# Dividing 2-D attention by its softmax sums after the value product, with the factors passed through DRAM

## The chip, the cores and the metric

The kernel runs on one core of one Trainium2 chip. That core has five engines with a queue of instructions each: TensorE (PE in the profile: matrix products and transposes; PEld is its weight loads), VectorE (DVE), ScalarE (ACT), GpSimd (POOL) and SyncE (SP, which here only issues transfers). Transfers between DRAM and the on-chip memory run on 16 DMA engines. An engine takes its instructions in order; an instruction that must wait holds up all behind it on its engine. The metric is device time in microseconds (us), lower is better.

## The reference

One encoder block on 1024 positions of width 1024, in float32. After a modulated norm, one projection gives queries, keys and values for two attention branches and two gates. Branch A is a dilated attention with 8 heads, branch B a 2-D neighbourhood attention with 8 heads of width 64. Their outputs are projected, gated, added and projected again; then come a second norm, a ConvFFN and a last norm. The change is in branch B:

```python
def neighbourhood_attention_2d(q, k, v, rpb):
    ...                       # rows = 16, GRID_W = 64; a window of 8 rows x 16 columns, clamped to the grid
    s = jnp.einsum('brqhd,brakhd->bhrqak', q5, kr).astype(jnp.float32) * scale + bias[None]
    s = jnp.where(col_mask[:, None, :], s, -jnp.inf)
    p = jax.nn.softmax(s, axis=(-2, -1))
    o = jnp.einsum('bhrqak,brakhd->brqhd', p.astype(v.dtype), vr)
    return o.reshape(B, S, H, Dh)
```

The softmax is an exponential divided by its sum over a query's keys. Since the sum is one number for each query and head, the division can be made in p or, with the same result up to rounding, in o.

## The kernel before, in words

Products of full accuracy are made from split operands: a float32 number is the sum of a high part (`hi`) and a low part (`lo`), and a product is three matmuls, hi\*hi, hi\*lo and lo\*hi (lines 84 to 86 in `product`). ACT makes a high part by copying, DVE or POOL the low part by subtracting.

The attention of both branches is written out slot by slot. A slot is one pass of the loop at line 1378 over `slots[s]`, 0 to 101; within a slot the phases run in the order `settle`, early, first, O, T, one step of fill, S, last, and the rest of the fill. Jobs are put in by `at(slot, phase, job)`; `later(n, job)` puts a job in the early phase n slots on. All five engines follow this written order here (lines 851 and 853). The fill is another task, the projections of the gates (`fill_steps`, line 1318): three matmuls a step (lines 84 to 86), two steps a slot up to slot 63, three in slots 64 to 95, one in slots 96 to 101, and 17 more after the last slot (line 1443). Work of other engines that has no fixed place (output sums, splitting of values and weights) goes through `aside`, which hands it out by a credit of 550 ns for each fill step; `ensure` forces it out when it is needed.

The 2-D heads run in slots 64 to 101: head h starts at slot s0 = 64 + 4h (`NaHead`, line 1207). The queries are cut into four column blocks `cb` of 16 columns (256 queries each) and two halves R of 128 queries, and a block has 288 or 384 keys for a half. For each head:

- slots s0 to s0+3, phase S: `scores` of blocks 0, 3, 1, 2 (line 1260, PE). The next slot's `settle` runs `soft`: DVE adds the bias and takes the maximum (line 1270), ACT takes the exponential and its sum (line 1272; the sum lands in `st[:, 1]`).
- two slots after its scores, phase first: `normalise` (line 1275) of that block: DVE takes the reciprocal of two columns of sums (line 1277), then half R = 0 is multiplied on POOL and half R = 1 on DVE (line 1280), in place in P.
- slots s0+4 to s0+7, phase T: `turn` transposes P on PE (line 1289) into one of two PSUM banks `T`; the next `settle` splits it, high part on ACT (line 878), low part on DVE (line 882), which frees the bank.
- slots s0+7 and s0+9, phase O: `out` multiplies with the values (line 930, PE). Its two halves are added into the output tile `oT` by ACT (line 1309) and DVE (line 1313). A tile `oT` holds two heads, on partitions 0 to 63 and 64 to 127; after the second head it goes to DRAM (`o_scr`, line 1315), from where the next stage loads it (`o_load`, line 1411, tile `oraw`).

SP issues the loads in the same written order: for the next heads the queries and keys (line 402), values (line 777) and bias (line 1248), for the fill the weights (line 65) and the store of its results (line 1327), for branch A its last factors (lines 1145 to 1203, up to slot 85). POOL has, beside line 1280, the low parts of the values (line 784) and of the fill's weights (line 962) and the weighting of branch A (lines 1193 and 1201).

After the slots come the gated products (`pj<-o0hi,whi` in the profile) and the ConvFFN. Behind line 1543, where the written order ends, a planner that simulates the engines' times orders most engines anew, with some stretches written out again.

Of the kernel before, what the change touches and what calls it, by code (L numbers as in the profile page):

```python
# [10 lines left out]
FT = mybir.dt.float32  # L11
FR = mybir.dt.float32r
AF = mybir.ActivationFunctionType
OP = mybir.AluOpType
# [3 lines left out]
S = 1024  # L18
# [10 lines left out]

def hybrid_encoder(tc, xT, c, w_ada, small, w_in, p1_bias, p23_bias, na_bias, ln2_mult, ident, w_br, w_out,  # L30
                   w_up, w_down, out):
    nc = tc.nc
    act, dve, pool, pe, sp = nc.scalar, nc.vector, nc.gpsimd, nc.tensor, nc.sync
# [3 lines left out]
    dram = tc.alloc_tile_pool(name="scr", bufs=1, space=DRAM)  # L37
# [89 lines left out]
    early = tc.alloc_tile_pool(name="early", bufs=1, reuse_waits="tile")  # L127
# [9 lines left out]
    later = itertools.cycle([(adapool, "wada", 4)] * 4 + [(early, "wada", 3)] * 3)  # L137
# [143 lines left out]
    g_scr = dram.tile([16, 128, S], FT, name="gs")  # L281
    st_scr = dram.tile([4, 64, 128], FT, name="sts")
    f_scr = dram.tile([4, 2, 2, 8, S], FT, name="fcs")
    o_scr = [dram.tile([4, 128, S], FT, name=n) for n in ("oa", "ob")]
    v_scr = dram.tile([S + 9 * 128, 512], FT, name="v")
    va_s, va_b = v_scr[:S], v_scr[S:].rearrange("(j p) n -> j p n", j=9)
# [14 lines left out]
    def v_wide(*sts):  # L301
        ps = [ps_s.tile([128, 512], FT, name="pv", bufs=3) if len(sts) == 1 else ps_g.tile([128, 512], FT, name="pj")
              for _ in sts]
        for k in range(KT):
            whi, wlo = (t[:, :, k] for t in v_all)
            for st, p in zip(sts, ps):
                hhi, hlo = (t[:, st % 4 * 128:st % 4 * 128 + 128] for t in h[st // 4, k])
                pe.matmul(p, hhi, whi, start=k == 0, stop=False)
                pe.matmul(p, hhi, wlo, start=False, stop=False)
                pe.matmul(p, hlo, whi, start=False, stop=k == KT - 1)  # L310
        return ps
# [83 lines left out]
    def qk_load(head):  # L395
        pr, i = divmod(head, 2)
        a = slice(64 * i, 64 * i + 64)
        qk = [qk2.tile([128, S], FR, name=n) for n in ("qs", "ks", "kl")]
        for y in range(3):
            rows = f(qk[y]).rearrange("(p b) s -> b p s", b=2)  # L400
            for b in range(2):
                sp.dma_start(rows[b], q_scr[pr, 1 + y if y else b, a])
        return qk
# [122 lines left out]
    with tc.manual_schedule(engines={e.engine for e in (sp, act, dve, pool, pe)}):  # L526
# [28 lines left out]
        r, eps = rt[:, :4], rt[:, 4:5]  # L555
# [24 lines left out]
        for q in range(4):  # L580
# [16 lines left out]
            last = 6 if q else 5  # L597
# [129 lines left out]
        for n, step in enumerate(v_steps[:10]):  # L727
# [18 lines left out]
            else:  # L746
                p = v_wide(*step[1:])
# [99 lines left out]
    qk2 = tc.alloc_tile_pool(name="qk2", bufs=2, reuse_waits="tile")  # L847
# [27 lines left out]
    def split_t(pt, then, m=128, n=512):  # L875
        def one():
            tt = [at_pool.tile([128, 512], FR, name=x_, bufs=5) for x_ in ("th", "tl")]
            act.activation(tt[0][:m, :n], pt[:m, :n], AF.Copy)  # L878
            return tt

        def two(tt):
            dve.tensor_tensor(tt[1][:m, :n], pt[:m, :n], f(tt[0])[:m, :n], OP.subtract)  # L882
            then(tt)
        turned.append((one, two))
# [12 lines left out]
    def aside(ns, one=lambda: None, two=lambda: None):  # L897
        side.append((ns, one, two))
        count[0] += 1
        return count[0]  # L900

    def flush():
        while second:
            second.popleft()()
            count[1] += 1

    def emit():
        ns, one, two = side.popleft()
        one()
        second.append(two)  # L910
        return ns
# [7 lines left out]
    def ensure(mark):  # L919
        while count[1] < mark:  # L920
            if not second:
                emit()
            flush()
# [25 lines left out]
    o_marks, o_count = [], [0]  # L949

    def o_tile():
        if o_count[0] > 1:
            ensure(o_marks[o_count[0] - 2])
        o_count[0] += 1
        return ps_a.tile([128, 512], FT, name="O")
# [15 lines left out]
    def at(slot, phase, job, *args):  # L971
        slots[slot][phase].append((job, args))
# [3 lines left out]
    def later(n, job):  # L976
        if now[0] + n > LAST:
            tail.append(job)
        else:
            at(now[0] + n, "early", job)  # L980
# [133 lines left out]
    class DilPair:  # L1114
# [22 lines left out]
        def turn(self):  # L1137
            pt = ps_a.tile([128, 512], FT, name="T")
            pe.transpose(pt[:64, :128], self.st.rearrange("p s i b -> p (s i b)"), idt)
            turned.append((lambda: None, lambda _: self.rows(pt)))  # L1140
# [66 lines left out]
    class NaHead:  # L1207
        def __init__(self, head, s0):
            self.head, self.i = head, head % 2
            self.a = slice(64 * self.i, 64 * self.i + 64)  # L1210
            self.P, self.t3, self.bt = {}, {}, {}
            at(57 if head == 0 else s0 - 4, "first", lambda: qks.update({8 + head: qk_load(8 + head)}))
            at(s0, "first", self.begin)
            at(s0 + 2, "first", self.load)
            at(s0 + 6, "first", self.output)
            at(s0 + 5, "first", self.prepare)
            for n, cb in enumerate((0, 3, 1, 2)):
                at(s0 + n - 2, "first", self.bias, cb)
                at(s0 + n, "S", self.scores, cb)
                at(s0 + n + 2, "first", self.normalise, cb)  # L1220
            for n, pair in enumerate(((0, 3), (1, 2))):
                s = s0 + 4 + 2 * n
                for y in range(3):
                    at(s + (y == 2), "T", self.turn, pair, y)
                at(s + 3, "O", self.out, pair)
# [49 lines left out]
        def normalise(self, cb):  # L1275
            st, P, kn = self.st, self.P[cb], 48 * NA_NC[cb]
            dve.reciprocal(st[:, 1, 2 * cb:2 * cb + 2], st[:, 1, 2 * cb:2 * cb + 2])
            for R in range(2):
                pp = P[:, R, :kn]
                (pool, dve)[R].tensor_scalar(pp, pp, st[:, 1, 2 * cb + R:2 * cb + R + 1], None, OP.mult)  # L1280

        def turn(self, pair, y):
            m = 16 * NA_NC[pair[0]]
            cb = pair[y % 2]
            spots = ([(cb, 0, 0), (cb, 1, 0), (cb, 1, 1), (cb, 3, 1)] if y < 2 else
                     [(pair[0], 2, 0), (pair[0], 2, 1), (pair[1], 2, 0), (pair[1], 2, 1)])
            pt = ps_a.tile([128, 512], FT, name="T")
            for x_, (cb, g, R) in enumerate(spots):
                pe.transpose(pt[:m, 128 * x_:128 * x_ + 128], self.P[cb][:, R, m * (g - R):m * (g - R) + m], idt)  # L1289
            split_t(pt, lambda tt: self.t3.update({(pair, y): tt}), m)  # L1290

        def out(self, pair):
            m = 16 * NA_NC[pair[0]]
            ensure(self.mark)
            t3 = [self.t3.pop((pair, y)) for y in range(3)]
            po = o_tile()
            for y, cb in enumerate(pair):
                turned_products(po, [(self.vv[:m, 4 * cb + g], [t[:m, c0:c0 + n] for t in tt],
                                      slice(256 * y + d0, 256 * y + d0 + n)) for g, tt, c0, d0, n in
                                     ((1, t3[y], 128, 0, 256), (2, t3[2], 256 * y, 0, 256), (0, t3[y], 0, 0, 128),  # L1300
                                      (3, t3[y], 384, 128, 128))], True)
            oT = oTs[self.head // 2]
            parts = [(oT[self.a].rearrange("p (r w t) -> p w r t", r=4, w=16)[:, :, :, 4 * cb:4 * cb + 4],
                      po[:, 256 * y:256 * y + 256].rearrange("p (w r t) -> p w r t", w=16, r=4))
                     for y, cb in enumerate(pair)]

            def one():
                for dst, pv in parts:
                    act.activation(dst, pv[64:128], AF.Copy)

            def two():
                for dst, pv in parts:
                    dve.tensor_tensor(dst, pv[0:64], dst, OP.add)
                if self.i and pair == (1, 2):
                    later(1, lambda: sp.dma_start(o_scr[1][self.head // 2], oT))
            o_marks.append(aside(800, one, two))

    def fill_steps():
        w, raw = first_w, {1: ahead.pop(25)}
# [35 lines left out]
                    yield  # L1355
            w = w_next

    oTs, w_raw = {}, {}
    for pr in range(4):
        DilPair(pr)  # L1360
    for head in range(8):
# [16 lines left out]
    for s in range(LAST + 1):  # L1378
        now[0] = s
        n = 2 if s < 64 else 3 if s < 96 else 1  # L1380
# [18 lines left out]
    o = [[opool.tile([128, 4, S], FR, name=f"o0{n}") for n in ("hi", "lo")]]  # L1399
# [114 lines left out]
    for i in range(2 * KT):  # L1514
# [17 lines left out]
        p = []  # L1532
# [296 lines left out]
    with tc.manual_schedule(engines={act.engine, dve.engine, pool.engine}):  # L1829

        def scale(k):
            dve.tensor_tensor(m2[k], m2[k], bc, OP.mult)
# [69 lines left out]
    for t in range(2, FF):  # L1902
# [9 lines left out]
        for c, j in enumerate(gens[t] if t < 3 else up_products(t, sts[t])):  # L1912
# [5 lines left out]
            if t == FF - 2 and j == 6:  # L1918
                first = a_operands(down_load(*jobs[0]), G, s_home, down_sts[0], apart=True)
# [54 lines left out]
    with tc.manual_schedule(engines={dve.engine}):  # L1974
        for hf, cs in ((0, slice(0, 512)), (1, slice(0, 256)), (1, slice(256, 512))):
            n = cs.stop - cs.start
            late = []
            for m in range(KT):
                if hf == 0 and m + 2 < KT:
                    end_w[m + 2] = end_weights(m + 2)  # L1980
                p = ps.tile([128, 512], FT, name="pj", bufs=6)[:, :n]
# [20 lines left out]
            r = wpool.tile([128, KT], FT, name="rs", bufs=2)[:, :n // 128]  # L2002
# [13 lines left out]
        dst = out[:, :, halves[hf]][:, :, cs]  # L2016
# [110 lines left out]
```

## Time and profile before

| | us |
|---|---|
| median of 3 runs | 1456.46 |
| lowest and highest | 1453.87, 1459.68 |
| the profiled execution, its own time | 1457.42 |
| span of the profiled execution | 1455.6 |
| PE busy in the span | 1430.4 |
| scores of the 2-D heads, first and last start | 466.4, 593.4 |
| divisions in P, first and last start | 472.3, 598.1 |
| granted TensorE clock | 0.998 |

Times in a view are counted from the start of the span. A row of groups reads: line, engine, operation, output tile <- input tiles, partitions x elements, count | busy us, mean ns of one | idle time of the engine just before them and what ended it. A row of the timeline reads: start, duration, engine, line, operation, tiles, count of merged instructions, and in brackets the idle time before. PE's matmuls are pipelined, so their durations overlap.

### The profile page before, as it was taken

The numbers are of one execution on the slowest core, as the hardware profiler recorded it, in microseconds if no ns is written. First come the engines' busy times: TensorE is split into PE (matmuls) and PEld (weight loads), VectorE is DVE, ScalarE is ACT, GpSimd is POOL, SyncE is SP. The second block draws the span as 40 slices with busy tenths as digits, with TensorE's granted clock in tenths as the row PEclk, the third lists the DMA queues.
The fourth block names the chain that finished last, engine by engine and source line by source line (L and its number), as shares of the span: only waits on it lengthen the run. The fifth ranks groups of instructions, "written<-read, shape, count | busy, mean of one in ns | idle before, by whom it ended". The sixth has DMA issues, their size and how long they took to land.

```text
span 1455.6 us, 21205 instructions
## 1 busy us (share of the span) xinstructions
PE 1430.4 (98%) x7276; PEld 1207.1 (83%) x7276; DVE 952.3 (65%) x1793; ACT 793.0 (54%) x1479; POOL 860.2 (59%) x707
## 2 busy tenths in 40 slices
PE   9999999999999999999999999999999999999998
PEld 8888788888888888887888778888888888887787
DVE  7687454365656766666418997666666668787865
ACT  6625543288887676644345554444444448575542
POOL 4156675343663675422478588677666676988712
PEclk9999999999999999999999999999999999999999
DMA  9587244676776797587444122222222233642313
GB/s 369 215 330 256 101 174 171 214 218 179 227 235 198 243 299 249 167 293 246 160 159 148 62 87 90 84 87 87 87 87 87 87 138 105 216 139 65 113 36 116
DMA packets 131498, 241.11 MB, mean 166 GB/s; under 512 B 48640, under 2 KB 62592, under 8 KB 131328
## 3 DMA queue, kind: packets, MB, share of 16 engines
q1 hardware_dynamic: 122304, 219.26, 46.0%
q10 hardware_dynamic: 9088, 20.52, 3.7%
q8 instruction: 57, 0.93, 0.3%
q14 instruction: 49, 0.40, 0.1%
HBM read 185.34 MB, written 60.16 MB: 169 GB/s over the span
## 4 chain that ended last, share of the span: by engine, by line
PE 71%; DVE 9%; DMA 7%; POOL 6%; ACT 3%; issue 3%; SPq 0%; ACTq 0%; DVEq 0%; POOLq 0%
PE pj L499 13%; PE pj L497 13%; PE pj L498 13%; PE pj L84 7%; PE pj L85 7%; PE pj L86 7%; PE O L930 3%; POOL wlo L61 2%; DMA oraw<-w_ada 2%; PE T L1289 1%; PE S L1260 1%; DMA wraw<-w_down 1%; PE T L1047 1%; DVE op L1661 1%; PE S L1070 1%
## 5 line engine op out<-in xcount | busy, mean ns | idle before, releaser
L61 POOL TENSOR_TENSOR wlo<-wraw,whi 128x512 fp32r<-128x512 f32 (+1 forms) x90 | 113.7, 1284 | 126.1 <-ACT whi L57 111.8
L497 PE MATMUL pj<-op,wsh 128*128 128x512 f32 x408 | 158.5, 390 | 1.6 <-ACT wsh L57 1.6
L498 PE MATMUL pj<-op,wsh 128*128 128x512 f32 x408 | 158.7, 389 | 0.4 <-DVE op L1550 0.4
L499 PE MATMUL pj<-op,wsl 128*128 128x512 f32 x408 | 157.4, 389 | 0.0
L61 POOL TENSOR_TENSOR wsl<-big,wsh 128x512 fp32r<-128x512 f32 (+1 forms) x86 | 111.7, 1320 | 45.0 <-ACT wsh L57 39.8
L84 PE MATMUL pj<-h,whi 128*128 128x512 f32 x272 | 115.1, 423 | 0.0
L86 PE MATMUL pj<-h,wlo 128*128 128x512 f32 x272 | 106.9, 393 | 0.0
L85 PE MATMUL pj<-h,whi 128*128 128x512 f32 x272 | 106.7, 392 | 0.0
L1760 DVE SCALAR_TENSOR_TENSOR big<-pj,sm,big 128x512 f32<-128x512 f32 (+2 forms) x183 | 94.9, 563 | 16.5 <-ACT big L1754 15.6
L497 PEld LDWEIGHTS pj<-op,wsh 128*128 128x128 f32 x408 | 76.6, 188 | 18.3 <-ACT wsh L57 2.4
L497 PE MATMUL pj<-op,whi 128*128 128x512 f32 x232 | 90.7, 391 | 0.3 <-ACT wc L503 0.3
L498 PE MATMUL pj<-op,whi 128*128 128x512 f32 x232 | 90.5, 390 | 0.2 <-DVE op L1580 0.2
L498 PEld LDWEIGHTS pj<-op,wsh 128*128 128x128 f32 x408 | 76.6, 188 | 16.9 <-DVE op L1550 0.9
L499 PE MATMUL pj<-op,wlo 128*128 128x512 f32 x232 | 90.3, 389 | 0.0
L499 PEld LDWEIGHTS pj<-op,wsl 128*128 128x128 f32 x408 | 76.6, 188 | 15.9 <-POOL wsl L61 0.2
L61 POOL TENSOR_TENSOR wsl<-wraw,wsh 128x384 fp32r<-128x384 f32 (+1 forms) x46 | 56.6, 1252 | 55.8 <-ACT wsh L57 50.2
L868 DVE CUSTOM_DVE_ANT_0 P<-S,bias 128x256 f32<-128x256 f32 x128 | 49.1, 421 | 61.2 <-PE S L1032 34.0
L882 DVE TENSOR_TENSOR tl<-T,th 128x512 fp32r<-128x512 f32 (+3 forms) x120 | 76.0, 649 | 8.6 <-ACT th L878 8.5
L57 ACT ACTIVATE whi<-wraw 128x1024 fp32r<-128x1024 f32 (+2 forms) x48 | 47.4, 992 | 57.7 <-PE pj L85 28.8
L869 ACT ACTIVATE P<-P,st 128x256 f32<-128x256 f32 x128 | 64.1, 502 | 26.0 <-DVE st L868 25.2
L962 POOL TENSOR_TENSOR wlo<-wraw,whi 128x512 fp32r<-128x512 f32 x30 | 38.6, 1294 | 64.6 <-ACT whi L961 61.1
L1754 ACT ACTIVATE big<-pj,sm 128x512 f32<-128x512 f32 x61 | 47.0, 772 | 54.3 <-DVE pj L518 32.2
(470 smaller groups left out, 4486.4 us busy)
## 6 DMA issues: line engine op xcount, KB each, us to landing
wada<-w_ada SPq DMA_DIRECT2D x31, 512.0 KB
qks<-qs ACTq DMA_DIRECT2D x28, 512.0 KB
wraw<-w_in SPq DMA_DIRECT2D x24, 512.0 KB
big<-w_up SPq DMA_DIRECT2D x22, 512.0 KB
wraw<-w_up SPq DMA_DIRECT2D x22, 512.0 KB
big<-as SPq DMA_DIRECT2D x22, 512.0 KB
as<-big SPq DMA_DIRECT2D x21, 512.0 KB
qs<-qks SPq DMA_DIRECT2D x32, 256.0 KB
```

The costliest lines, as they stand in the source:

```text
L57: act.activation(hi, raw, AF.Copy)
L61: lo_eng.tensor_tensor(lo[:, i:i + step], raw[:, i:i + step], f(hi)[:, i:i + step], OP.subtract)
L84: pe.matmul(psum, whi[:, k0 + k], mhi, start=k == 0, stop=False)
L85: pe.matmul(psum, whi[:, k0 + k], mlo, start=False, stop=False)
L86: pe.matmul(psum, wlo[:, k0 + k], mhi, start=False, stop=k == n - 1)
L497: pe.matmul(psum, whi[:, k], bhi, start=j < 4 and k == 0, stop=False, skip_group_check=True)
L498: pe.matmul(psum, whi[:, k], blo, start=False, stop=False, skip_group_check=True)
L499: pe.matmul(psum, wlo[:, k], bhi, start=False, stop=k == n - 1, skip_group_check=True)
L868: dve.tensor_tensor_reduce(pp, d, bias, -1.0, BIG, OP.add, OP.min, mi)
L869: act.activation(pp, pp, AF.Exp, bias=mi, scale=-1.0, accum_out=li)
L882: dve.tensor_tensor(tt[1][:m, :n], pt[:m, :n], f(tt[0])[:m, :n], OP.subtract)
L1760: dve.scalar_tensor_tensor(y[:, dst], src, wt, y[:, dst], OP.mult, OP.add)
```

## The change

The six first 2-D heads no longer divide P. Their sums are inverted once for all four blocks, in slot s0+5 (`inverse`: one DVE reciprocal of 128 x 8 numbers); one slot later SP stores the 1024 factors to DRAM, in the order of the queries (`i_scr`), in slot s0+8 it loads them back, each spread over the 64 partitions of the head (`load_inverse`, into a tile `qb` that branch A no longer uses). When both heads of an output tile are done, POOL multiplies the tile by the factors (`scale`: four products of 128 x 256, one for each column block, in slots s0+11 and s0+12 of the odd head), and the store of the tile follows a slot later. The last two heads, 6 and 7, divide as before.

```diff
@@ -281,6 +281,7 @@
     f_scr = dram.tile([4, 2, 2, 8, S], FT, name="fcs")
+    i_scr = dram.tile([8, S], FT, name="is")
@@ -1217,7 +1218,14 @@
             for n, cb in enumerate((0, 3, 1, 2)):
                 at(s0 + n - 2, "first", self.bias, cb)
                 at(s0 + n, "S", self.scores, cb)
-                at(s0 + n + 2, "first", self.normalise, cb)
+                if head > 5:
+                    at(s0 + n + 2, "first", self.normalise, cb)
+            if head < 6:
+                at(s0 + 5, "first", self.inverse)
+                at(s0 + 8, "early", self.load_inverse)
+                if self.i:
+                    for cb in range(4):
+                        at(s0 + 11 + cb // 2, "last", self.scale, cb)
@@ -1278,6 +1286,26 @@
+        def inverse(self):
+            st = self.st
+            dve.reciprocal(st[:, 1], st[:, 1])
+            later(1, lambda: sp.dma_start(i_scr[self.head].rearrange("(e p) -> p e", p=128), st[:, 1]))
+
+        def load_inverse(self):
+            if self.i == 0:
+                inv[self.head // 2] = qk2.tile([128, S], FT, name="qb")
+            sp.dma_start(inv[self.head // 2][self.a],
+                         i_scr[self.head].rearrange("(o n) -> o n", o=1).to_broadcast([64, S]))
+
+        def scale(self, cb):
+            ensure(self.done)
+            pr = self.head // 2
+            dst = oTs[pr].rearrange("p (r w t) -> p w r t", r=4, w=16)[:, :, :, 4 * cb:4 * cb + 4]
+            by = inv[pr][:, 256 * cb:256 * cb + 256].rearrange("p (w r t) -> p w r t", w=16, r=4)
+            pool.tensor_tensor(dst, dst, by, OP.mult)
+            if cb == 3:
+                later(1, lambda: sp.dma_start(o_scr[1][pr], oTs[pr]))
@@ -1311,9 +1339,10 @@
-                if self.i and pair == (1, 2):
+                if self.i and pair == (1, 2) and self.head > 5:
                     later(1, lambda: sp.dma_start(o_scr[1][self.head // 2], oT))
-            o_marks.append(aside(800, one, two))
+            self.done = aside(800, one, two)
+            o_marks.append(self.done)
@@ -1355,7 +1384,7 @@
-    oTs, w_raw = {}, {}
+    oTs, inv, w_raw = {}, {}, {}
```

## The prediction

> **What bounds the kernel now.** I read the shares of the page first, then a table by stage, then what PE waited for in the stage that changes.
>
> ```profile
> PE 1430.4 (98%) x7276; PEld 1207.1 (83%) x7276; DVE 952.3 (65%) x1793; ACT 793.0 (54%) x1479; POOL 860.2 (59%) x707
> ```
>
> ```profile
> core 0: us, PE busy (x) PEld busy (x) DVE busy (x) ACT busy (x) POOL busy (x), PEclk, DMA share, GB/s
> 463.00:609.00 146.00, 141.79 (x929) 125.67 (x928) 98.49 (x293) 102.12 (x272) 87.76 (x78) 1.00 0.75 238
> 609.00:626.00 17.00, 17.00 (x77) 14.08 (x76) 10.54 (x14) 13.36 (x22) 3.00 (x2) 1.00 0.94 318
> ...
> 700.00:1000.00 300.00, 297.25 (x1327) 244.23 (x1327) 200.29 (x288) 143.41 (x189) 214.10 (x157) 1.00 0.31 104
> 1000.00:1300.00 300.00, 299.77 (x1323) 247.87 (x1322) 207.51 (x329) 155.21 (x221) 219.20 (x181) 1.00 0.33 112
> 1300.00:1456.00 156.00, 146.83 (x758) 124.49 (x756) 105.77 (x165) 71.12 (x128) 82.28 (x82) 0.98 0.29 93
> ```
>
> The 2-D heads lie in 463 to 609. PE is uncovered there for 146.00 - 141.79 = 4.2 us; DVE and POOL, the engines that divide, are idle for 47 and 58 us. So PE bounds the stage, and an edit that moves no matmul can win only out of 4.2 us. The waits of PE that the profile names, over 463 to 620:
>
> ```profile
> PE T L1289 <- DVE stb L1277: 3.1, 3, 1.5
> PE O L930 <- issue: 0.7, 1, 0.7
> PE T L1289 <- POOL vv L784: 0.4, 1, 0.4
> ```
>
> Three waits of transposes, 3.1 us, are put down to the reciprocal. The other 1.1 us belong to head 7 (they fall behind 600 us), which keeps its division. The timeline of the three, of PE, DVE, ACT and POOL:
>
> ```profile
> 495.27 0.62 PE L1289 MATMUL T<-idt,P 128*96 128x128 f32 x4 [0.79 <-DVE stb L1277]
> 504.87 0.63 PE L1289 MATMUL T<-idt,P 128*128 128x128 f32 x4 [1.48 <-DVE stb L1277]
> 563.03 0.61 PE L1289 MATMUL T<-idt,P 128*96 128x128 f32 x4 [0.80 <-DVE stb L1277]
> ```
>
> ```profile
> 494.43 0.69 DVE L882 TENSOR_TENSOR tl<-T,th 128x512 fp32r<-128x512 f32 x1 [0.95 <-ACT th L878]
> ...
> 500.69 2.68 DVE L1171 TENSOR_TENSOR fa<-fa,fl 64x32 f32<-64x32 f32 x2
> ...
> 504.05 0.68 DVE L882 TENSOR_TENSOR tl<-T,th 96x512 fp32r<-96x512 f32 x1
> ...
> 562.20 0.69 DVE L882 TENSOR_TENSOR tl<-T,th 128x512 fp32r<-128x512 f32 x1 [0.96 <-ACT th L878]
> ```
>
> ```profile
> 493.14 0.63 ACT L961 ACTIVATE whi<-wraw 128x512 fp32r<-128x512 f32 x1 [1.61 <-PE pj L85]
> ```
>
> ```profile
> 499.27 1.41 POOL L1280 TENSOR_SCALAR P<-P,stb 128x384 f32<-128x384 f32 x1 [1.25 <-DMA qs<-qks]
> ...
> 500.65 2.67 POOL L784 TENSOR_TENSOR vv<-vv 96x256 fp32r<-96x256 f32 x3
> ```
>
> Each transpose starts 0.14 to 0.15 us after an L882 ends (494.43 + 0.69, 504.05 + 0.68, 562.20 + 0.69), and L882 frees the PSUM bank that the transpose needs. The reciprocal merely stands next on DVE. In the first and third case L882 itself waited 0.95 us for the high part on ACT, which stood behind a weight split that had waited 1.61 us for PE (the 493.14 row; I take the third to be the same, both L882 rows having the same wait). The division is not in that chain. Only the second goes through it in part: two tiny DVE products take 2.68 us while POOL works on values that came late behind a division of 1.41 us.
>
> **The change part by part.** Removed for heads 0 to 5, so 24 of 32 blocks:
>
> ```profile
> L1280 POOL TENSOR_SCALAR P<-P,stb 128x288 f32<-128x288 f32 (+1 forms) x32 | 39.4, 1233 | 43.8 <-DVE stb L1277 23.6 <-ACT P L1272 10.7 <-PE O L930 3.6
> ```
>
> ```profile
> L1280 DVE TENSOR_SCALAR P<-P,stb 128x288 f32<-128x288 f32 (+1 forms) x32 | 15.5, 484 | 1.1
> ...
> L1277 DVE RECIPROCAL stb<-stb 128x2 f32<-128x2 f32 x32 | 4.9, 153 | 0.0
> ...
> L1171 DVE TENSOR_TENSOR fa<-fa,fl 64x32 f32<-64x32 f32 x2 | 2.7, 1378 | 0.0
> ```
>
> POOL: 24 x 1.233 = 29.6 us. DVE: 24 x (0.484 + 0.153) = 15.3 us. Neither is on the path, save for the 504.87 wait. There DVE is free 0.57 us earlier (0.42 + 0.15 for one block) and POOL's values can start up to 1.4 us earlier. I take a gain of 0.8 us of that wait's 1.48. Bounds for all waits: 0 (the same banks are late) and 3.1 us (all three go).
>
> By the Trainium skill (SBUF — State Buffer, the section on who contends), a DVE instruction with two inputs in SBUF and a GpSimd instruction that reads SBUF exclude each other for a whole instruction. The 1.378 us of the 64x32 products beside POOL's values agree with it. By that rule fewer POOL instructions mean fewer such stalls, so the gain would be all of the 504.87 wait, 1.5 us.
>
> Added on DVE: 6 reciprocals of 128x8. The 128x2 one takes 0.153 us; six are about 1 us, in idle time. Added on POOL: 12 products of 128x256 with runs of four numbers. No row has such runs on POOL. The nearest:
>
> ```profile
> L784 POOL TENSOR_TENSOR vv<-vv 96x256 fp32r<-96x256 f32 x16 | 11.9, 741 | 0.0
> ...
> L1201 POOL TENSOR_TENSOR u<-u,u 128x512 f32<-128x512 f32 x4 | 5.2, 1290 | 0.0
> ```
>
> I take 0.8 us (the first, same count per partition); ends 0.74 and, if short runs cost as much as twice the numbers, 1.29. So POOL does 9.6 us (8.9 to 15.5) in place of 29.6. Nothing of it is on the path except perhaps in the last slots (below).
>
> Added on SP and the DMA engines, for each of six heads: a store of 1024 single numbers and a load of 64 rows of 4 KB. Prices of many small pieces, from SP's issues and from a stretch (584 to 589 us) with value loads almost alone:
>
> ```profile
> L681 SPq DMA_DIRECT2D vv<-v x8: 378/412/542, 283.4 to 434.3; - x8
> ```
>
> ```profile
> L1188 SPq DMA_DIRECT2D fb<-fcs x32: 574/590/652, 357.4 to 535.6; - x32
> ```
>
> ```profile
> q1 hardware_dynamic: 1856, 0.46, 40.6%
> ```
>
> ```profile
> q1 hardware_dynamic: 28497, 35.33, 74.3%
> ```
>
> L681 issues 128 x 8 = 1024 pieces in 0.41 us; L1188 is a broadcast load like the new one. So SP gets 6 x (0.41 + 0.59) = 6 us more. A 256-byte piece costs 0.406 x 5 x 16 / 1856 = 17.5 ns of one DMA engine; the mean packet of the whole stage (second row, 460 to 610 us) 0.743 x 150 x 16 / 28497 = 62.6 ns. A store is 64 pieces for each engine: 1.1 us by the nearer row, which I take; 4.0 by the farther; 0 if it is all latency. The load is 4 rows for each engine, 0.25 us by that mean, or 0.83 by its bytes (a row has 3.3 times the mean packet's 35.33 MB / 28497 = 1240 B); I take 0.4. Six heads: 6 x 1.5 = 9 us (1.5 to 29) of 16 engines whose share in 463 to 609 is 0.75, so about 0.81. That costs nothing as long as loads come early enough. The first and the last scores give the length of a slot:
>
> ```profile
> L1260 PE MATMUL S<-ks,qs x64: 291/320/343, 466.4 to 593.4; 128*128 128x288 f32 x32, 128*128 128x384 f32 x32
> ```
>
> (593.4 - 466.4) / 31 = 4.1 us. SP can issue the store when the reciprocal of slot s0+5 is done, and wants the load at s0+8: two slots or 8 us for 1024 numbers to land. POOL wants the factors at s0+11, three more slots. If the store lands late, SP stands, and behind it are the biases of the head two further on (line 1248, needed two slots later), fill results and weights. So the cover is 8 us before SP stands at all and 16 before a bias is late; without it each us over 16 is a us of DVE's scores and soon of PE, for six heads.
>
> The Trainium skill (DMA: Bandwidth & Descriptors, rules for kernel authors) speaks against this store: a last dimension that isn't contiguous becomes one descriptor per element, and it advises a layout with a contiguous last dimension. No transfer of before has 4-byte runs; the 17.5 ns pieces say that a thousand descriptors are cheap, so the sum would be the same by the rule unless each costs many times that.
>
> Moved: the store of an output tile goes from slot s0+10 to s0+13 of the odd head, past three slots of SP's queue, and now waits for POOL in place of DVE. The tile has no other user before the next stage. Only the third tile is near its reader, in the short slots 95 to 97:
>
> ```profile
> 595.61 1.37 POOL L1280 TENSOR_SCALAR P<-P,stb 128x384 f32<-128x384 f32 x1 [2.98 <-ACT P L1272]
> 598.15 1.37 POOL L1280 TENSOR_SCALAR P<-P,stb 128x384 f32<-128x384 f32 x1 [1.17 <-DVE stb L1277]
> 599.49 2.68 POOL L784 TENSOR_TENSOR vv<-vv 96x256 fp32r<-96x256 f32 x3
> ```
>
> ```profile
> 596.52 1.83 SPq L1413 DMA_DIRECT2D oraw<-oa  x4
> ```
>
> ```profile
> 609.84 2.19 ACT L1420 ACTIVATE o0hi<-oraw 128x512 fp32r<-128x512 f32 x4 [0.41 <-ACT gs L1325]
> ```
>
> Behind the 595.61 division (ends 596.98) come two products, to 598.6 (or 599.6 at 1.29 each), so the 598.15 division and the values of head 7 slip by 0.4 us (1.4). PE needs those at once: 0.2 us loss, up to 1.4. SP's store then leaves at 598.6, and the loads behind it, at 596.52 before, 2.1 us later; ACT uses them at 609.84, over 8 us after: no cost.
>
> Behind line 1543 the planner may order anew, since its simulated times move. No row prices that; PE's uncovered time from 700 us on is 2.75 + 0.23 + 9.17 = 12.2 us, so a gain is below that. For a loss I take the same 12.2 as the end. Value taken: 0, since no work there is changed.
>
> Sum: -0.8 (transposes) + 0.2 (last slots) + 0 (DMA) + 0 (order behind) = -0.6 us, against the profiled execution's 1457.42, so 1456.8. That execution is 0.96 us over the median of the runs shown; the forecast in terms of the median is 1456.46 - 0.6 = 1456 us.
>
> **The rivals.** *All waits go.* If the views' word is right and the reciprocal holds all three transposes, the gain is 3.1 us: 1453.4. For it: the releaser named. Against: the L882 ends. Still no change within 0.5% (7.3 us, about what a measurement of this kernel can tell from no change).
>
> *The factors' trip is late (slower).* Place: SP's wait between store and load. Price: each us of landing over 16 us, six times. It decides from a landing of 16 us; at 18 us it is 6 x 2 = 12 us, so 1468. For it: the DMA share, 0.75 already, and no 4-byte runs known. Against: 17.5 ns a piece; even 62.6 ns make 4 us.
>
> *The order behind attention changes.* 1468.7 to 1444.3 by the ends above; typically a few us, which is no change. For it: lines 1543 on are planned from simulated times. Against: PE is 99% covered from 700 to 1300 us.
>
> *The division doesn't shorten anything at all, and the last slots lose.* With 1.29 us products and no gain: +1.4, 1457.9, no change.
>
> **How the numbers follow.** Forecast (-0.6, within 3 us): 0.58. All waits go: 0.10. Last slots lose: 0.08. Order behind: 0.17, of which 0.06 slower and 0.06 faster by over 0.5%, 0.05 within. Late factors: 0.07, of which 0.06 slower by over 0.5%. So faster 0.06, slower 0.12, no change 0.82. The likeliest one's own range is 1453 to 1460; the range that reaches to the others up to half of the re-ordering's ends is 1449 to 1465.
>
> **What would show it.** Right: in 463 to 609 PE is uncovered for 3 to 4.5 us still; the transpose waits of about 0.8 us behind an L882 that waited for ACT stand as before, the third is shorter; POOL there is 20 us less busy and DVE 14; the new POOL product takes about 0.8 us and doesn't wait for its factors; SP's wait ahead of the load is under 2 us. Wrong: transposes with no wait at all, a PE wait behind POOL's products or behind biases, a store that takes over 8 us, or PE's uncovered time behind 700 us off by several us.

## The result and the profile after

The changed kernel takes 1493.74 us (median; 1490.31 to 1499.09), beside 1456.19 us for the kernel before: a ratio of 1.0248, 95% interval 1.023 to 1.0266. That is 37.6 us slower, outside the predicted range.

The span grew from 1455.6 to 1487.7 us, by 32.1 us. Two lines of the page of the kernel after, the busy times and the granted TensorE clock in 40 slices:

```profile
PE 1439.3 (97%) x7276; PEld 1214.6 (82%) x7276; DVE 937.8 (63%) x1751; ACT 793.6 (53%) x1479; POOL 838.0 (56%) x695
...
PEclk9999999999999988999999999999999999999999
```

With the same 7276 matmuls PE is 8.9 us longer busy (1439.3 - 1430.4), and its uncovered time grew from 25.2 to 48.4 us, by 23.2; together they are the 32.1. The table by stage of the kernel after (columns as in the prediction: stretch, its length, busy times, clock, DMA share, GB/s) says where:

```profile
463.00:609.00 146.00, 122.91 (x744) 107.86 (x744) 67.20 (x203) 83.95 (x223) 49.52 (x49) 0.93 0.89 212
...
540.00:580.00 40.00, 27.88 (x152) 24.26 (x151) 13.58 (x41) 17.38 (x48) 13.78 (x14) 0.79 0.94 207
```

```profile
700.00:1400.00 700.00, 694.48 (x3075) 571.88 (x3073) 481.16 (x722) 351.40 (x494) 495.80 (x398) 1.00 0.34 115
```

and the same long stretch of the kernel before:

```profile
700.00:1400.00 700.00, 695.10 (x3074) 571.58 (x3074) 484.58 (x725) 353.09 (x504) 498.70 (x401) 1.00 0.32 106
```

Behind 700 us nothing changed: PE is busy for 694.5 against 695.1 us. Nor did it up to 463 us (455.4 against 455.2). All of the loss lies among the 2-D heads, where PE is now uncovered for 23.1 us of the first 146, against 4.2. The largest groups of waits there, of PE and of DVE (each row: engine, tile and line that waited, what it waited for; us in total, times, longest):

```profile
PE T L1317 <- DVE tl L883: 27.1, 9, 9.0
...
DVE P L1278 <- DMA bias<-na_bias: 30.3, 4, 12.4
```

(L1317, L883, L1278 and L1256 are the lines 1289, 882, 1270 and 1248 of before.) The longest single wait, followed back through the timelines of PE, DVE and SP:

```profile
574.75 1.06 PE L1317 MATMUL T<-idt,P 128*96 128x128 f32 x4 [9.03 <-DVE tl L883]
```

```profile
573.16 0.46 DVE L1278 CUSTOM_DVE_ANT_0 P<-S,bias 128x288 f32<-128x288 f32 x1 [12.39 <-DMA bias<-na_bias]
...
573.92 1.28 DVE L883 TENSOR_TENSOR tl<-T,th 96x512 fp32r<-96x512 f32 x2
```

```profile
552.96 0.37 SPq L1293 DMA_DIRECT2D is<-stb  x1
553.44 9.37 SPq L778 DMA_DIRECT2D vv<-vb  x4
562.85 0.48 SPq L1256 DMA_DIRECT2D bias<-na_bias  x1
...
563.85 0.43 SPq L1256 DMA_DIRECT2D bias<-na_bias  x1
569.52 0.53 SPq L1298 DMA_DIRECT2D qb<-is  x1
```

Read from the last of the three: at 552.96 SP issues a store of 1024 factors. The next four issues, the value loads of another head, take 9.37 us; four such issues of before are

```profile
554.83 2.55 SPq L777 DMA_DIRECT2D vv<-vb  x4
```

The bias behind them goes out at 562.85 and is not there until about 573. DVE stands for 12.39 us at the scores that need it; behind that, in order, stands L883, which frees the PSUM bank of the next transpose; PE waits 9.03 us.

SP's issues were slow while the DMA path was. This is the DMA share in 40 slices of 510 to 517.5 us in the kernel after, 4 us behind another store, with the queue's packets, MB and share:

```profile
DMA  9939419301111010011100022000000000000030
...
q1 hardware_dynamic: 461, 0.05, 22.0%
```

For some 6 us almost nothing moves, though SP has transfers to issue. And 555.2 to 569.5 us, behind the store of 552.96:

```profile
q1 hardware_dynamic: 2415, 0.75, 89.9%
```

A packet takes 0.899 x 14.3 x 16 / 2415 = 85 ns of a DMA engine, for 310 bytes on average; before, the 256-byte pieces took 17.5 ns.

### The profile page after: what moved, and what is told of

Read it like the earlier page. It is cut to its first block, busy times and chain, and to the rows that moved or that the text cites. A ratio compares the mean times of both kernels' runs of the same rounds, so it can differ in the third digit from the quotient of the medians.

```text
span 1487.7 us, 21175 instructions
## 1 busy us (share of the span) xinstructions
PE 1439.3 (97%) x7276; PEld 1214.6 (82%) x7276; DVE 937.8 (63%) x1751; ACT 793.6 (53%) x1479; POOL 838.0 (56%) x695
## 4 chain that ended last, share of the span: by engine, by line
PE 49%; DVE 3%; ACT 2%; POOL 1%; issue 1%; DMA 1%; SPq 0%; DVEq 0%; ACTq 0%; POOLq 0%
PE pj L498 11%; PE pj L499 11%; PE pj L500 11%; PE pj L86 5%; PE pj L84 5%; PE pj L85 5%; DMA oraw<-oa 0%; DMA wraw<-w_br 0%; DVE big L463 0%; POOL wlo L61 0%; DVE op L1690 0%; ACT wsh L57 0%; ACT op L1608 0%; DMA wraw<-w_down 0%; PE pcol L108 0%
## 5 line engine op out<-in xcount | busy, mean ns | idle before, releaser
L84 PE MATMUL pj<-h,whi 128*128 128x512 f32 x272 | 117.3, 431 | 0.0
L85 PE MATMUL pj<-h,whi 128*128 128x512 f32 x272 | 108.5, 399 | 0.0
L1789 DVE SCALAR_TENSOR_TENSOR big<-pj,sm,big 128x512 f32<-128x512 f32 (+2 forms) x183 | 94.9, 562 | 16.5 <-ACT big L1783 15.6
L785 POOL TENSOR_TENSOR vv<-vv 128x512 fp32r<-128x512 f32 (+2 forms) x40 | 43.0, 1096 | 85.5 <-ACT vv L784 79.2
L883 DVE TENSOR_TENSOR tl<-T,th 128x512 fp32r<-128x512 f32 (+3 forms) x120 | 76.0, 649 | 8.7 <-ACT th L879 8.5
L870 ACT ACTIVATE P<-P,st 128x256 f32<-128x256 f32 x128 | 64.0, 502 | 25.9 <-DVE st L869 25.2
```

What stands on the lines that cost most here:

```text
L84: pe.matmul(psum, whi[:, k0 + k], mhi, start=k == 0, stop=False)
L85: pe.matmul(psum, whi[:, k0 + k], mlo, start=False, stop=False)
L870: act.activation(pp, pp, AF.Exp, bias=mi, scale=-1.0, accum_out=li)
L1789: dve.scalar_tensor_tensor(y[:, dst], src, wt, y[:, dst], OP.mult, OP.add)
```

## The experiments

Theory 1: the 1024 writes of four bytes clog the path to DRAM, and loads that come after them are late. Theory 2: the trip is the cause, SP standing at the load until the store has landed. Theory 3: the products on POOL or the later store of the outputs. Ratios are against the kernel before on the same chip.

| kernel | median us | before, us | ratio | 95% interval |
|---|---|---|---|---|
| store alone, packed (4 bytes apart) | 1488.56 | 1457.67 | 1.0223 | 1.0195 to 1.0251 |
| store alone, 64 bytes apart | 1458.55 | 1457.67 | 1.0004 | 0.999 to 1.0018 |
| no division in six heads | 1456.50 | 1457.67 | 0.9994 | 0.9982 to 1.0006 |
| all of the change, runs of eight numbers | 1458.09 | 1457.67 | 1.0002 | 0.9989 to 1.0014 |
| store alone, packed, from ACT's queue | 1485.09 | 1456.42 | 1.0202 | 1.0184 to 1.022 |
| store alone, 8 bytes apart, lines of their own | 1476.05 | 1456.42 | 1.0143 | 1.0124 to 1.0161 |
| store alone, 8 bytes apart, order of the queries | 1464.61 | 1456.42 | 1.0058 | 1.0043 to 1.0073 |
| store alone, packed, three heads | 1465.11 | 1456.42 | 1.0064 | 1.0049 to 1.0079 |
| lines of their own, 1 KB apart | 1497.31 | 1458.66 | 1.0272 | 1.0254 to 1.0289 |
| store alone, 16 bytes apart | 1458.85 | 1458.66 | 1.0003 | 0.9992 to 1.0014 |

### The store alone

```diff
 # the kernel before, NaHead
                 at(s0 + n + 2, "first", self.normalise, cb)
+            if head < 6:
+                at(s0 + 6, "early", self.keep)
+        def keep(self):
+            sp.dma_start(i_scr[self.head].rearrange("(e p) -> p e", p=128), self.st[:, 1])
```

> The kernel before, all heads dividing in P, with only the store of the 1024 factors of heads 0 to 5 added in slot s0+6; nothing reads them. Theory 1 (the 1024 writes of four bytes themselves keep the DMA path busy for about 10 us a head, and loads behind them come late): most of the 37.6 us appear, 1480 to 1495 us. Theory 2 (SP stands at the load until the store has landed, and what is queued behind is late): nothing stands at the store, so 1456, within 5. Theory 3 (the products on POOL, or the store of the outputs three slots later): 1456, within 5.

It took 1488.56 us, 30.9 over the kernel before. Most of the loss comes from a store that nothing reads: no load, no product, no wait for a landing. The waits are those of the changed kernel:

```profile
DVE P L1273 <- DMA bias<-na_bias: 34.2, 6, 8.2
...
PE T L1295 <- DVE tl L883: 21.7, 6, 5.5
```

Theory 1 stands; 2 and 3 can't be the main cause. The intervals of this kernel (1.0195 to 1.0251) and of the changed one (1.023 to 1.0266) overlap, so what the trip adds is not told apart from nothing here.

### The same store, 64 bytes apart

```diff
-    i_scr = dram.tile([8, S], FT, name="is")
+    i_scr = dram.tile([8, 16 * S], FT, name="is")
-  i_scr[self.head].rearrange("(e p) -> p e", p=128)
+  i_scr[self.head].rearrange("(e p x) -> p e x", p=128, x=16)[:, :, 0]
```

> As the store alone, but every number goes to its own 64 bytes (a step of 64 bytes in place of four). If the four-byte writes are slow because many of them fall into the same few bytes of DRAM, this is fast, 1456 within 5. If each small write costs by itself, it is as slow as the store alone (1480 to 1495), or slower. Theories 2 and 3: 1456.

1458.55 us, ratio 1.0004: nothing. The same number of pieces, of the same four bytes, from the same partitions, issued at the same place. PE's waits are back to those of before:

```profile
PE T L1295 <- DVE stb L1280: 3.1, 3, 1.5
```

So small pieces as such cost this kernel nothing, as the prediction had it. What costs is where they land.

### The division left out

```diff
-                at(s0 + n + 2, "first", self.normalise, cb)
+                if head > 5:
+                    at(s0 + n + 2, "first", self.normalise, cb)
```

> The kernel before with the divisions of heads 0 to 5 left out and nothing in their place (these heads' outputs are not divided by their sums): the removed part alone. By the prediction's step it gains 0 to 3.1 us, 0.8 taken: 1453 to 1457. If the division had held the transposes at all three waits: 1453.

In this kernel the outputs of heads 0 to 5 stay undivided. It takes 1456.50 us, ratio 0.9994: the whole gain there was to be had can't be told from none. In its trace PE waits, over 463 to 609 us:

```profile
PE T L1290 <- DVE tl L882: 0.9, 1, 0.9
PE T L1290 <- DVE fl L1159: 0.8, 1, 0.8
PE O L930 <- issue: 0.7, 1, 0.7
PE T L1290 <- POOL vv L784: 0.4, 1, 0.4
```

The two transposes of 0.8 us that the prediction put down to ACT's weight split are there without any division (0.9 and 0.8); the L882 ahead of each waited 1.12 and 1.07 us for the high part on ACT. The third, 1.48 us before, is gone. The two tiny DVE products ahead of it (L1171), 1378 ns each before, are now short, but another one two instructions earlier (L1168), 184 ns before, is long in their place:

```profile
L1168 DVE TENSOR_TENSOR fl<-fs 64x32 f32<-64x32 f32 x1 | 2.0, 1996 | 0.0
L1171 DVE TENSOR_TENSOR fa<-fa,fl 64x32 f32<-64x32 f32 x2 | 0.4, 230 | 0.0
```

POOL's work on the values (three products, 2.68 us) now starts 3.86 us behind the first of the transpose waits (499.81 against 495.95) in place of 5.38 (500.65 against 495.27). So DVE's stall beside it is still there and only comes earlier. Between the two waits that stay the kernel is 1.4 us shorter (495.95 to 562.31, against 495.27 to 563.03).

### The change with runs of eight numbers

```diff
-  i_scr[self.head].rearrange("(e p) -> p e", p=128)
+  i_scr[self.head].rearrange("(p e) -> p e", p=128)
-            by = inv[pr][:, 256 * cb:256 * cb + 256].rearrange("p (w r t) -> p w r t", w=16, r=4)
-            pool.tensor_tensor(dst, dst, by, OP.mult)
+            by = inv[pr].rearrange("p (w r t e) -> p e w r t", w=8, r=4, t=4)
+            for R in range(2):
+                d = dst[:, 8 * R:8 * R + 8]
+                pool.tensor_tensor(d, d, by[:, 2 * cb + R], OP.mult)
```

> The changed kernel, but the factors are stored in runs of eight numbers (128 pieces of 32 bytes), and the products on POOL pick them by a step of eight (eight products of 128x128 for each tile in place of four of 128x256). Theory 1: 1456 within 6, the loss is gone though store, load, waits and products are all there. Theory 2: the trip is there as before, so 1485 to 1495. Theory 3: 1485 or more.

1458.09 us, ratio 1.0002. With the eight factors of a partition side by side in DRAM the store is 128 pieces of 32 bytes in place of 1024 of four; slots, load, waits, products and the later output store are all there, and the loss is gone. It does not beat the kernel before. Its stage and its products on POOL:

```profile
463.00:609.00 146.00, 142.49 (x937) 126.32 (x936) 84.93 (x255) 102.19 (x273) 71.28 (x78) 1.00 0.81 252
```

```profile
L1308 POOL TENSOR_TENSOR u<-u,qb 128x128 f32<-128x128 f32 x24 | 12.4, 546 | 0.0
```

PE is uncovered for 3.5 us (4.2 before), POOL 16.5 and DVE 13.6 us less busy. A product here has half the numbers of one in the changed kernel and takes 546 ns against 729, so each number costs 1.5 times as much.

### From ACT's queue

```diff
-            sp.dma_start(i_scr[self.head].rearrange("(e p) -> p e", p=128), self.st[:, 1])
+            act.dma_start(i_scr[self.head].rearrange("(e p) -> p e", p=128), self.st[:, 1])
```

> The store alone (added to the kernel before, nothing reads it), issued from ACT's queue in place of SP's. If the loads are late because they stand behind the store in SP's own queue, the loss goes: 1457 to 1461. If the memory path behind all queues is clogged, it stays: 1480 to 1495.

1485.09 us, 28.7 over before. The loads on SP's queue are late even when the store is not on it, by nearly as much (34.2 us with the store on SP's own):

```profile
DVE P L1273 <- DMA bias<-na_bias: 30.0, 6, 7.9
```

So it is not the order in SP's queue: a store from ACT's queue clogs the path for SP's transfers too.

### Which writes meet: lines of their own, or shared

Both runs put the numbers 8 bytes apart, so each 64 bytes of DRAM get eight writes in place of sixteen; in the first all eight come from one partition.

```diff
-    i_scr = dram.tile([8, S], FT, name="is")
+    i_scr = dram.tile([8, 2 * S], FT, name="is")
 # lines of their own
+  i_scr[self.head].rearrange("(p e x) -> p e x", p=128, x=2)[:, :, 0]
 # order of the queries
+  i_scr[self.head].rearrange("(e p x) -> p e x", p=128, x=2)[:, :, 0]
```

> The store alone, four bytes a piece as before, but with the eight numbers of a partition side by side, 8 bytes apart: each 64 bytes of DRAM get eight writes, all from one partition and so from one DMA engine. Theory A (writes to the same 64 bytes queue behind one another, whoever sends them): still slow, half as many for each 64 bytes, 1468 to 1490. Theory B (it is several DMA engines that write the same bytes at once): fast, 1457 within 5.

> The store alone, 8 bytes apart as in the run with lines of their own, but in the order of the queries: each 64 bytes get eight writes from eight partitions, so from more than one DMA engine. Theory A: as slow as the other. Theory B: slow, 1468 to 1495, where the other is fast. If both are fast, only the packed order of four bytes is slow.

1476.05 us (19.6 over) and 1464.61 us (8.2 over). Theory B falls: the writes of a single partition into its own bytes are slow too, even slower than when several partitions share the bytes. Theory A holds as far as both are slow; it did not foresee that they differ. The difference fits writes that follow each other directly into the same bytes, which is the case in the first and not in the second, but no run shows the order in which they arrive.

### Three heads

```diff
-            if head < 6:
+            if head in (0, 2, 4):
                 at(s0 + 6, "early", self.keep)
```

> The store alone, for heads 0, 2 and 4 only. If each store costs for itself, half of the loss of six: 1457.7 + 15 = 1473, within 5. If the loss comes from stores that meet the loads of a certain stretch, or piles up from one to the next, well off half: under 1465 or over 1481.

1465.11 us, 8.7 over, against 15.5 for half of six; that is between the two ranges expected, next to the lower. The stores do not simply add up. That fits loads which are issued slots ahead: the first microseconds of a clog fall into their lead, and with twice the time between stores the lead can grow again. This is an argument; no run shows the lead itself.

### Few KB, or the same 64 bytes

```diff
-    i_scr = dram.tile([8, S], FT, name="is")
+    i_scr = dram.tile([8, 256 * 128], FT, name="is")
+  i_scr[self.head].rearrange("(p e x) -> p e x", p=128, x=2)[:, 0:8, 0]
```

> The store alone as in the run with lines of their own (eight writes of one partition, 8 bytes apart, into 64 bytes), but each partition's 64 bytes stand 1 KB from the next, so that the 128 of them cover 128 KB in place of 8 KB. If it counts that eight writes go to the same 64 bytes: the loss of that run stays, 1472 to 1480. If it counts that a thousand writes fall into a few KB of DRAM (the packed store covers 4 KB, the fast one of single numbers 64 bytes apart covers 64 KB): gone, 1457 within 4.

1497.31 us, 38.7 over: not better but twice as bad as the same lines packed into 8 KB. So the loss doesn't need a thousand writes in a few KB. Eight writes into the same 64 bytes are slow in both layouts; that a step of 1 KB between them makes it worse was not expected and is not explained. No run has single writes 1 KB apart, so a cost of that step by itself is not excluded.

### 16 bytes apart

```diff
+  i_scr[self.head].rearrange("(e p x) -> p e x", p=128, x=4)[:, :, 0]
```

> The store alone in the order of the queries, 16 bytes apart (four writes for each 64 bytes, 16 KB covered); 4 bytes apart cost 31 us, 8 bytes 8 us, 64 bytes nothing. If the loss goes on falling with the writes for each 64 bytes: under 4 us, 1456 to 1460. If writes within 64 bytes cost by their number and cover hid the rest at 8 bytes: 0 as well; over 1464 would speak against both.

1458.85 us, ratio 1.0003. In the order of the queries the loss goes 31, 8, 0, 0 us for 4, 8, 16 and 64 bytes apart. One wait for a bias is left in this trace, and none at 64 bytes:

```profile
DVE P L1273 <- DMA bias<-na_bias: 0.6, 1, 0.6
```

Are four writes for each 64 bytes quick, or is the clog only short enough for the cover? SP's own issues tell. Two to four us behind the second store SP issues eight small transfers to DRAM. Before, they take 2.80 us in all:

```profile
504.27 2.80 SPq L1181 DMA_DIRECT2D fcs<-fa  x8
```

They also take 2.80 us in the run with three heads, which leaves out just this store. Behind the store 64 bytes apart they take 3.47 us, at 16 bytes 4.46, at 8 bytes 4.91 in the order of the queries and 6.93 in lines of their own, packed 11.48, and 12.02 with 1 KB between the lines; with the packed store on ACT's queue 6.71. So at 16 bytes SP is still slowed, and it stays hidden; a little of that is left even at 64 bytes.

## Why the prediction was wrong

**What bounds the kernel, and what the division costs**: right. PE bounds the stage; of the three transpose waits two have nothing to do with the division (the run without it keeps them at 0.9 and 0.8 us), and the third does. Its gain was taken at 0.8 us; without the division the view of waits no longer lists it, so the gain there was nearly all of the 1.48. The prediction's 1.5 came from another reading: that fewer POOL instructions mean fewer stalls of DVE. The long stall stayed: DVE still stands beside POOL's values, now in L1168 (1996 ns), only earlier, because no division stands ahead of the values. The rule behind that reading (the Trainium skill, SBUF — State Buffer, Who interferes with whom) is that a DVE instruction with two SBUF inputs and a GpSimd instruction that reads SBUF exclude each other. With POOL's values both traces agree. With POOL's divisions the trace of before doesn't: L1168 takes 184 ns there although a division of 1.41 us runs (499.27 to 500.68; a trace is rough on POOL's spans).

**POOL and DVE**: right. The group of new products in the kernel after:

```profile
L1306 POOL TENSOR_TENSOR u<-u,qb 128x256 f32<-128x256 f32 x12 | 8.5, 729 | 0.0
```

729 ns against 0.8 us taken; runs of four numbers cost POOL nothing. They never waited for their factors (0.0). Over the whole span POOL is 22.2 and DVE 14.5 us less busy; 20 and 14 were forecast for the stage.

**The store of 1024 numbers**: this is the step that failed. It priced the store by what its pieces take of the DMA engines, "1.1 us by the nearer row", and went on that this "costs nothing as long as loads come early enough". The time of the pieces was no trap: stores 64 bytes apart, with as many pieces, cost the kernel nothing. Even the packed pieces are quick by themselves: from ACT's queue, where they can be read alone, 1040 packets take 9.1% of 16 engines in 485.6 to 492 us, 9 ns each, half of the 17.5 taken. What was missing is a term that no row of before could show, because no transfer there writes four-byte pieces: behind a packed store the path to DRAM is clogged for SP's transfers, whether SP or ACT issued the store, for some 6 us in one of the stretches above and 14 in the other (85 ns a packet in place of 17.5, four of SP's issues at 9.4 us in place of 2.6). The upper bound, 4.0 us for each store from the mean packet of the stage, was an end for the wrong quantity.

**The slower rival** had the place nearly right and the mechanism wrong. It asked whether the factors' own landing would hold up SP, and let it decide at 16 us. For two heads SP did stand at the load until the store had landed:

```profile
SPq L1298 <- DMA is<-stb: 9.7, 2, 5.2
```

By SP's timeline these two stores went out at 530.80 and 552.96 and their loads at 542.00 and 569.52, so they took about 11 and 16.6 us. Both are over the 8 us that the prediction named as a sign of being wrong, and the second reached the rival's point. But the loss is there with no load at all; it is the other heads' values and biases that are late, at any landing time, and the cover of two slots that the prediction counted for a bias was spent before it was issued (DVE stood at its scores from 560.8, the bias went out at 562.85). It had a chance of 0.07.

The rule that was weighed (the Trainium skill, DMA: Bandwidth & Descriptors, rules for kernel authors: a last dimension that isn't contiguous becomes one descriptor per element, so rearrange it) was set aside because descriptors are cheap. They are; the advice was right all the same, and following it (runs of eight) removes the loss. The same page of the Trainium skill (Specifications) says that a transfer below 512 bytes makes the DMA engine read, modify and write. If each four-byte write reads and writes back a larger block, writes into one block must wait for each other; that fits the runs by spacing, but none shows the reads: the pages of before and of the store alone both give 185.34 MB read from DRAM.

**The order behind attention**: right, no change (694.5 against 695.1 us). **The last slots**: in the run with runs of eight PE has two waits in place of the one of 0.42 us of before, 0.57 and 0.55, so 0.7 us more in all, between the 0.2 us taken and its end of 1.4:

```profile
PE T L1319 <- POOL P L1288: 0.6, 1, 0.6
PE O L931 <- POOL vv L785: 0.6, 1, 0.6
```

**The range**: half of the re-ordering's 12.2 us on either side gives 1450 to 1463; the 1449 and 1465 that were written are a little wider.

Open: how large the block is in which writes meet, why one partition's writes are slower than several partitions', and why 1 KB between the blocks makes it worse.

## What to carry to other kernels

Price a transfer not only by its own pieces but by what it does to the transfers behind it: a store that nobody reads cost 31 us here. When factors leave with one number for each partition and column, store them in the order in which a partition holds them and rearrange in the access pattern of the reader; eight side by side made 1024 writes into 128 and took the loss to nothing. And before moving work off an engine, look whether its instruction ends last in a wait: here removing it from six of eight heads gained nothing that could be measured.

## What the runs showed of the hardware

Six stores of 1024 four-byte writes, close together in DRAM, hold up SP's later transfers, whether SP or ACT issues them. Counted by the writes into each 64 bytes (a way of counting; no run measured the block), 16 cost this kernel 31 us; 8, between 8 and 20 us, or 39 with 1 KB between the blocks; 4 or fewer in the order of the queries, nothing, though SP's issues behind them are still slower (4.46 and 3.47 us against 2.80).

PE's waits cost more than their length. The table by stage of the kernel after, right behind the 9.03 us wait:

```profile
574.70:578.00 3.30, 3.25 (x12) 2.96 (x13) 1.00 (x4) 2.48 (x8) 2.81 (x3) 0.50 1.03 313
578.00:581.00 3.00, 3.00 (x16) 2.48 (x15) 1.88 (x7) 1.81 (x6) 2.44 (x4) 0.70 1.05 373
581.00:585.00 4.00, 4.00 (x29) 3.62 (x28) 2.25 (x6) 2.21 (x6) 0.00 (x0) 1.00 1.18 119
```

The granted clock is 0.50 for 3.3 us and comes back within the next 3: 12 matmuls in the first stretch, 29 in 4 us at full clock. The 8.9 us by which the same matmuls take longer in the span fit this: the mean clock of 463 to 609 us is 0.93. It agrees with the Trainium skill (TensorE: Matmul & The Clock Gate, Part 1), by which the clock halves after an idle window of about 3.4 us and returns after about as long of sustained work.
